# A two-layer decoder trunk: first product's first two units interleaved, six convolution taps moved to TensorE, layer norm read from PSUM

## The chip, the cores and the metric

The kernel runs on one core of one Trainium2 chip. The metric is the device time of one execution in microseconds (us). A core has five engines that run side by side, each with its own queue of instructions, worked off in order: TensorE (PE, matrix products; its weight loads are shown as PEld), VectorE (DVE), ScalarE (ACT), GpSimd (POOL) and SyncE (SP, which here issues the transfers). They work on the on-chip memory SBUF; TensorE writes to PSUM, eight banks of 2 KB a partition, which DVE and ACT can read and write too. An instruction waits on semaphores for what it needs.

## What is computed

The input x is 256 positions by 2048 channels in float32. Cut to what matters here, with the attention of the second layer and both feed-forward stages left as they are:

```python
def _conformer_conv(h, w1, b1, dw, dw_b, ln_g, ln_b, w2, b2):
    u = h @ w1 + b1
    a, gate = jnp.split(u, 2, axis=-1)
    u = a * jax.nn.sigmoid(gate)
    u = lax.conv_general_dilated(u, dw[:, None, :], ...) + dw_b
    u = jax.nn.silu(_layernorm(u, ln_g, ln_b))
    return u @ w2 + b2
...
h = h + _conformer_conv(_rmsnorm(h, a_norm_g), ...)
h = h + _swiglu(_rmsnorm(h, ffn_norm_g), ...)
h = h + _dilated_attention(...) @ w_o
h = h + _swiglu(_rmsnorm(h, ffn_norm_g), ...)
return _rmsnorm(h, final_norm_g)
```

## The kernel before

Activations lie transposed, channels on the 128 partitions: 16 tiles of 128 x 256. Each weight matrix is cut into units (256 output columns) and a unit into blocks of 512 KB: four tiles of 128 input channels. One list, `blocks` (L120 to L143), holds all blocks in the order in which they are used. `emit_block` (L149) loads the next one into `raw` (four buffers, on SP's queue) and parts it into `whi` (float32r, rounded, a copy on ACT) and `wlo` (the rest, a subtraction on DVE or POOL), three buffers each; it runs two blocks ahead of its use. A tile of weights then takes three passes on TensorE: whi with x's high part, whi with x's low part, wlo with x's high part. The first product's first block of a unit is native: float32 weights and float32 x (`rawn`, `xf`, L240) in one pass, which needs no parting.

The first product (w1, line L245) has 16 units of 256 columns, each making a gate tile and a value tile of the same 128 channels. With unit 0 the activations are loaded too: `load_x` (L378) puts a piece of x before each piece of weights on SP's queue, parts x (L292 on ACT, L293 on DVE), and the squares for the RMS norm are summed on POOL, ACT and DVE (L311 to L315). The norm's factor (L318) is applied to the unit's result in PSUM (`glu`, L394). Then the unit's convolution runs while TensorE works on the next units: the taps (`conv`, L406) are shared by POOL and ACT (six products), DVE (the others, L426, accumulating in PSUM), and for the last unit TensorE (16 taps as products with diagonal matrices, L419). `later` and `tick` (L189, L192) deal out these pieces block by block. `stats` (L478) gathers mean and mean square in PSUM by products with a matrix of ones.

The layer norm (L521 to L547) is the seam: it needs all 16 tiles, and its instructions on ACT, DVE and POOL stand in the order in which they are written. It copies the mean to SBUF, subtracts it (DVE for the first two tiles, POOL for the others), multiplies by the reciprocal standard deviation (L537), applies SiLU (L545), and parts the result into z's high and low halves (L546, L547), which the second product (w2, L211 and L216 from here on) reads. Its eight units follow one after the other, each with a tile `pp` of two banks, two such tiles in all.

At the end the last product (wd1, L252) gives its outputs with positions on partitions, in two halves of 128 positions; for its last quarter of the columns the first half is finished first, and `done` (L680) closes the norm and stores it while TensorE makes the second.

The functions that the change touches:

## Time and profile before

| what | us |
|---|---|
| median of the runs (2196.13 to 2197.51) | 2196.61 |
| the profiled execution, its own time | 2197.23 |
| its span, first to last instruction | 2194.4 |
| PE busy | 2166.4 (99%) |
| DVE, ACT, POOL busy | 1378.2, 1063.2, 468.2 |

The span is what the profile's rows are counted in, from 0; 2.8 us of the execution's time lie outside it. A row in order of time has start, length, engine, line, operation, out<-in, shapes, how many instructions were merged and, in brackets, the idle time before and what ended it. Lengths overlap: the next instruction of an engine can start up to 0.1 us before the one ahead has ended, and a matmul's end is modelled, so the distance from start to start tells more. A float32 matmul is two records.

### The profile page before, as it was taken

How to read it: one execution, taken by the hardware profiler on the slowest of the kernel's cores; microseconds unless marked ns; L12 is line 12 of the kernel's file. 1: busy time of each engine (PE TensorE's matmuls, PEld its weight loads, DVE VectorE, ACT ScalarE, POOL GpSimd, SP SyncE). 2: the span in 40 equal slices, each digit the busy share in tenths (PEclk: the TensorE clock that was granted, in tenths of full speed). 3: DMA queues.
4: the chain of work that ended last, by engine and by line, in shares of the span. 5: the costliest groups of instructions: out<-in, count | busy, mean ns of one | idle time of the engine just before them, and what ended most of it. 6: DMA issues, size and time to landing. Idle time of an engine off the chain costs nothing.

```text
span 2194.4 us, 31099 instructions
## 1 busy us (share of the span) xinstructions
PE 2166.4 (99%) x12242; PEld 1903.6 (87%) x12242; DVE 1378.2 (63%) x1634; ACT 1063.2 (48%) x1381; POOL 468.2 (21%) x294
## 2 busy tenths in 40 slices
PE   8999799999999999999999999999999999999998
PEld 7999688888888888888888888888888888888886
DVE  7888876666666565555545677666666566655554
ACT  6666455444444444444444566554444444453333
POOL 5999211222221220000000100112221222210000
PEclk9999899999999999999999999999999999999999
DMA  6444355555555555555565644555655555565654
GB/s 235 168 170 154 105 186 189 183 192 185 191 190 192 192 191 185 191 192 191 178 195 187 192 142 144 183 185 186 191 187 192 192 192 191 185 194 194 196 190 155
DMA packets 112898, 402.40 MB, mean 183 GB/s; under 512 B 12656, under 2 KB 13680, under 8 KB 112752
## 3 DMA queue, kind: packets, MB, share of 16 engines
q1 hardware_dynamic: 111456, 398.30, 55.5%
q8 instruction: 95, 1.56, 0.3%
q10 hardware_dynamic: 1296, 2.12, 0.3%
q14 instruction: 51, 0.42, 0.1%
HBM read 398.28 MB, written 2.10 MB: 182 GB/s over the span
## 4 chain that ended last, share of the span: by engine, by line
PE 97%; DVE 1%; ACT 1%; issue 0%; DMA 0%; POOL 0%; SPq 0%; ACTq 0%; DVEq 0%
PE pp L211 47%; PE pp L216 25%; PE pp L245 8%; PE pp L263 5%; PE pp L265 5%; PE pp L264 5%; PE aux L608 0%; PE aux L613 0%; PE aux L590 0%; PE aux L489 0%; DMA hT<-xT 0%; ACT whi L171 0%; DVE aux L426 0%; PE aux L322 0%; DVE wlo L173 0%
## 5 line engine op out<-in xcount | busy, mean ns | idle before, releaser
L173 DVE TENSOR_TENSOR wlo<-raw,whi 128x1024 fp32r<-128x1024 f32 (+1 forms) x691 | 939.9, 1373 | 504.8 <-ACT whi L171 502.6
L171 ACT CAST whi<-raw 128x1024 fp32r<-128x1024 f32 (+1 forms) x739 | 773.6, 1048 | 789.9 <-PE pp L211 406.0
L211 PE MATMUL pp<-x,whi 128*128 128x512 f32 x3328 | 802.1, 392 | 0.0
L211 PEld LDWEIGHTS pp<-x,whi 128*128 128x128 f32 x3328 | 611.5, 188 | 117.4
L216 PEld LDWEIGHTS pp<-x,wlo 128*128 128x128 f32 x3328 | 426.9, 191 | 16.3
L216 PE MATMUL pp<-x,wlo 128*128 128x256 f32 x3328 | 433.2, 283 | 0.0
L287 DVE TENSOR_TENSOR t<-pp,t 128x512 f32<-128x512 f32 x104 | 71.9, 692 | 208.8 <-ACT t L286 208.8
L286 ACT COPY t<-pp 128x512 f32<-128x512 f32 x104 | 61.2, 588 | 259.8 <-PE pp L211 259.8
L568 POOL TENSOR_TENSOR hid<-t,hid 128x512 fp32r<-128x512 f32 x44 | 89.4, 2031 | 419.8 <-ACT hid L567 419.8
L211 PE MATMUL pp<-hid,whi 128*128 128x512 f32 x704 | 168.7, 391 | 0.0
L211 PEld LDWEIGHTS pp<-hid,whi 128*128 128x128 f32 x704 | 129.2, 188 | 24.9
L426 DVE SCALAR_TENSOR_TENSOR aux<-up,vecs,aux 128x256 f32<-128x256 f32 x355 | 144.7, 485 | 3.3 <-ACT aux L424 3.3
L245 PE MATMUL pp<-x,whi 128*128 128x256 f32 x768 | 143.8, 289 | 1.0 <-ACT whi L171 1.0
L315 POOL TENSOR_TENSOR sqacc<-sqacc,sq 128x512 f32<-128x512 f32 x24 | 36.2, 1507 | 505.6 <-ACT sq L311 505.4
L263 PE MATMUL pp<-whi,hid 128*128 128x512 f32 x352 | 137.8, 392 | 0.8 <-DVE x L669 0.8
L264 PE MATMUL pp<-wlo,hid 128*128 128x512 f32 x352 | 137.1, 389 | 0.4 <-DVE wlo L173 0.4
L265 PE MATMUL pp<-whi,hid 128*128 128x512 f32 x352 | 137.1, 389 | 0.0
L562 POOL TENSOR_TENSOR t<-t,rstd 128x512 f32<-128x512 f32 x44 | 57.0, 1295 | 316.5 <-DVE t L287 316.5
L245 PEld LDWEIGHTS pp<-x,whi 128*128 128x128 f32 x768 | 122.3, 194 | 2.3 <-ACT whi L171 1.4
L173 POOL TENSOR_TENSOR wlo<-raw,whi 128x1024 fp32r<-128x1024 f32 x48 | 114.0, 2389 | 24.4 <-DVE up L398 14.9
L245 PE MATMUL pp<-x,wlo 128*128 128x256 f32 x384 | 110.2, 287 | 3.2 <-DVE wlo L173 3.2
L216 PEld LDWEIGHTS pp<-hid,wlo 128*128 128x128 f32 x704 | 90.8, 191 | 3.7
(134 smaller groups left out, 1870.8 us busy)
## 6 DMA issues: line engine op xcount, KB each, us to landing
raw<-wg SPq DMA_DIRECT2D x176, 512.0 KB, 3.3
raw<-wu SPq DMA_DIRECT2D x176, 512.0 KB, 4.2
raw<-wd SPq DMA_DIRECT2D x176, 512.0 KB, 3.4
raw<-w SPq DMA_DIRECT2D x77, 512.0 KB, 3.2
raw<-wv SPq DMA_DIRECT2D x32, 512.0 KB, 4.0
raw<-wk SPq DMA_DIRECT2D x32, 512.0 KB, 4.2
raw<-wq SPq DMA_DIRECT2D x32, 512.0 KB, 3.4
raw<-wo SPq DMA_DIRECT2D x32, 512.0 KB, 3.3
```

What stands on the lines that cost most here:

```text
L171: nc.scalar.copy(hi[:, part, :], raw[:, part, :])
L173: eng.tensor_tensor(out=lo[:, part, :], in0=raw[:, part, :], in1=hi[:, part, :].bitcast(F32), op=ALU.subtract)
L211: nc.tensor.matmul(bk[:, m, :, :], hi[:, j, ws], x[:, kt, :, :], start=kt == 0, stop=kt == kt_n - 1 and m_last, skip_group_check=True)
L216: nc.tensor.matmul(bk[:, m, 0, :], lo[:, j, ws], x[:, kt, 0, :], start=False, stop=kt == kt_n - 1 and not m_last, skip_group_check=True)
L245: nc.tensor.matmul(bk[:, m, :], a[:, j, ws], b, start=first and m == 0 and i == 0, stop=last and i == len(passes) - 1, skip_group_check=True)
L263: nc.tensor.matmul(o, x[:, kt, 0, ts], hi[:, j, :], start=kt == 0, stop=False)
L264: nc.tensor.matmul(o, x[:, kt, 0, ts], lo[:, j, :], start=False, stop=False)
L265: nc.tensor.matmul(o, x[:, kt, 1, ts], hi[:, j, :], start=False, stop=kt == kt_n - 1)
L286: nc.scalar.copy(t, bk[:, :, 1, :])
L287: nc.vector.tensor_tensor(out=t, in0=bk[:, :, 0, :], in1=t, op=ALU.add)
L426: nc.vector.scalar_tensor_tensor(out=acc[i % 2], in0=win, scalar=w, in1=acc[i % 2], op0=ALU.mult, op1=ALU.add)
L568: nc.gpsimd.tensor_tensor(out=hid[:, 2 * u:2 * u + 2, 1, :], in0=o, in1=hid[:, 2 * u:2 * u + 2, 0, :].bitcast(F32), op=ALU.subtract)
```

## The change

Four things are changed.

1. The list of blocks begins with the first two units of w1 in turns (unit, block): `TURNS`. Both units' results are open at once, the second in a buffer of `aux`. The square sums use POOL for two pairs of x instead of four, unit 1's splits are on DVE, and the results of w1 have two banks instead of three.
2. Tile 14's convolution gives six of its taps to TensorE, with diagonal matrices as for tile 15. The table load for the square root is moved behind the products of tile 15.
3. The layer norm reads mean and reciprocal from the statistics' own PSUM bank (a pool `one` of one bank), DVE subtracts for the tiles 0 to 7 and POOL for 8 to 15, and the first two units of w2 run side by side: their first blocks are native (float32 weights with the float32 result of the SiLU), then their other blocks alternate, the second unit with its narrow pass first. Tiles 0 to 3 of z are parted last.
4. The last product's last quarter has two tiles of `aux` instead of one `pp`, and most of the norm's sum is prepared before it. `aux` has three buffers instead of four from the second product on; the attention's transposes use the bank of `one`.

TensorE at the start, before and after (pp is unit 0's result, aux unit 1's; rawn are native weights; L322 and L362 are the norm's sums):

```order
1 L245 MATMUL pp<-xf,rawn 128x256 x8
2 L245 MATMUL pp<-x,whi 128x256 x2
3 L245 MATMUL pp<-x,wlo 128x256
...
50 L322 MATMUL aux<-sqacc,cst 128x256 x2
51 L245 MATMUL pp<-xf,rawn 128x256 x8
```
```order
1 L259 MATMUL pp<-xf,rawn 128x256 x8
2 L259 MATMUL aux<-xf,rawn 128x256 x8
3 L259 MATMUL pp<-x,whi 128x256 x2
4 L259 MATMUL pp<-x,wlo 128x256
...
19 L259 MATMUL aux<-x,whi 128x256 x2
20 L259 MATMUL aux<-x,wlo 128x256
...
67 L362 MATMUL aux<-sqacc,cst 128x256 x2
```

Unit 1's native block stands second and its first split block (rows 19 on) ahead of unit 0's third block; its last two blocks come after row 67.

DVE at the layer norm, before and after (cT holds the 16 tiles, st the statistics in PSUM, rstd the factor; L533 and L608 are the reciprocal):

```order
185 L526 TENSOR_TENSOR rstd<-mu 128x256 [waits Activation_49]
186 L527 TENSOR_TENSOR rstd<-aux,rstd 128x256 [waits DVE_49,PE_49]
187 L532 TENSOR_TENSOR cT<-cT,mu 128x256 x2
188 L533 RECIPROCAL rstd<-rstd 128x256 [waits Activation_49]
189 L537 TENSOR_TENSOR cT<-cT,rstd 128x256 [waits DVE_49]
190 L537 TENSOR_TENSOR cT<-cT,rstd 128x256
191 L547 TENSOR_TENSOR z<-cT,z 128x256 [waits DVE_49,Activation_49]
192 L537 TENSOR_TENSOR cT<-cT,rstd 128x512 [waits Pool_49]
```
```order
171 L586 TENSOR_TENSOR cT<-cT,st 128x256 [waits PE_49,Activation_49]
172 L603 TENSOR_TENSOR rstd<-st,rstd 128x256
173 L586 TENSOR_TENSOR cT<-cT,st 128x256
174 L608 RECIPROCAL st<-rstd 128x256 [waits DVE_49,Activation_49]
175 L591 TENSOR_TENSOR cT<-cT,st 128x256 [waits DVE_49]
176 L591 TENSOR_TENSOR cT<-cT,st 128x256
177 L586 TENSOR_TENSOR cT<-cT,st 128x512
178 L591 TENSOR_TENSOR cT<-cT,st 128x512 [waits DVE_49]
```

Every one of DVE's operands that was mu or rstd in SBUF is now st in PSUM; z is parted only after row 182, and the wait for POOL stands later.

TensorE from the last taps into the second product, before and after (diag are the taps' matrices, L489, L493 and L539, L543 the statistics):

```order
877 L419 MATMUL aux<-up,diag 128x256 x15
878 L489 MATMUL aux<-cT,cst 128x256 [waits DVE_49]
879 L493 MATMUL aux<-sq_2607,cst 128x256 [waits Activation_49]
...
882 L211 MATMUL pp<-z,whi 128x512 [waits DVE_49,PE_49]
883 L211 MATMUL pp<-z,whi 128x512
884 L211 MATMUL pp<-z,whi 128x512 [waits DVE_49]
```
```order
824 L463 MATMUL aux<-up,diag 128x256 x5
...
881 L463 MATMUL aux<-up,diag 128x256 x15
882 L539 MATMUL st<-cT,cst 128x256 [waits DVE_49]
883 L543 MATMUL st<-sq_2626,cst 128x256 [waits Activation_49]
...
886 L272 MATMUL pp<-cT,rawn 128x256 [waits DMAHW4_49,PE_49,Activation_49]
...
888 L272 MATMUL pp<-cT,rawn 128x256 [waits Activation_49]
...
896 L284 MATMUL pp<-z,whi 128x512 [waits DVE_49]
...
900 L282 MATMUL pp<-z,wlo 128x256 [waits Pool_49]
```

Tile 14's six taps stand 57 rows earlier, among unit 15's matmuls; the second product now begins with matmuls that wait for ACT's SiLU alone, and DVE's parted z is first waited for in row 896.

The core of the diff:

```diff
-TAPS_OF = [(6, 0)] * 14 + [(6, 0), (3, 16)]
+TAPS_OF = [(6, 0)] * 14 + [(6, 6), (3, 16)]
...
-    for u in range(DT):
+    TURNS = ((0, 0), (1, 0), (0, 1), (1, 1), (0, 2), (0, 3), (1, 2), (1, 3))
+    blocks.extend((w1, u, g, GK) for u, g in TURNS)
+    for u in range(2, DT):
         plan(w1, u, DT)
-    for u in range(DT // 2):
+    for g in range(DT // GK):
+        blocks.extend((w2, u, g, GK) for u in range(2))
+    for u in range(2, DT // 2):
...
-        native = NATIVE if w is w1 and g == 0 else 0
+        native = NATIVE if g == 0 and (w is w1 or w is w2 and u < 2) else 0
...
-                eng = nc.gpsimd if (w is w1 and i >= 6) or (w is w2 and u == 0) else nc.vector
+                eng = nc.gpsimd if (w is w1 and u > 1) or (w is w2 and u < 2 and (u, g) in ((0, 1), (1, 1), (0, 2))) else nc.vector
...
+    one = ctx.enter_context(tc.tile_pool(name="one", bufs=1, space=PSUM))
...
-        return psum[-1].tile(shape, F32, name="aux", bufs=4 if len(psum) > 1 else 5)
+        return psum[-1].tile(shape, F32, name="aux", bufs=3 if len(psum) > 1 else 5)
...
+        bks = [aux([P, 2, S]) if i else psum[-1].tile([P, 2, S], F32, name="pp", bufs=2) for i in range(len(units))]
+        for u, g in TURNS if len(units) > 1 else [(0, g) for g in range(DT // GK)]:
+            raw, hi, lo = next_block(w, units[u], g)
...
+    def project_pair(w, xf, x, bks):
+
+        parts = [next_block(w, u, 0, 0)[0] for u in range(2)]
+        for s in range(0, GK, 2):
+            for bk, raw in zip(bks, parts):
+                for kt in (s, s + 1):
+                    for m in range(2):
+                        nc.tensor.matmul(bk[:, m, 0, :], raw[:, kt, m * P:(m + 1) * P], xf[:, kt, :], start=kt == 0, stop=False,
+                                         skip_group_check=True)
+            yield
+        for g in range(1, DT // GK):
+            for u, bk in enumerate(bks):
+                hi, lo = next_block(w, u, g, 0)[1:]
+                tiles = [(g * GK + j, j, m, slice(m * P, (m + 1) * P)) for j in range(GK) for m in range(2)]
+                for wide in ((True, False), (False, True))[u]:
+                    for kt, j, m, ws in tiles:
+                        if not wide:
+                            nc.tensor.matmul(bk[:, m, 0, :], lo[:, j, ws], x[:, kt, 0, :], start=False, stop=False, skip_group_check=True)
+                        else:
+                            nc.tensor.matmul(bk[:, m, :, :], hi[:, j, ws], x[:, kt, :, :], start=False, stop=kt == DT - 1,
+                                             skip_group_check=True)
+                yield
...
+        if done:
+            outs = [aux([P, NBV]) for _ in range(2)]
+        else:
+            bk = bank2()
+            outs = [bk[:, t, :, :].rearrange("p a b -> p (a b)") for t in range(2)]
...
-                norm.add(hT[:, j:j + 2, :], *((nc.gpsimd, nc.gpsimd) if j < DT // 2 else (nc.scalar, nc.vector)))
+                norm.add(hT[:, j:j + 2, :], *((nc.gpsimd, nc.gpsimd) if j < 4 else (nc.scalar, nc.vector)))
...
+            pe_acc = acc[-1]
+            begun = n_pe > 0 and j < DT - 1
...
-                if i < 2:
+                if i < 2 and not (i and begun):
...
+        table(AF.Sqrt, last_product[-1])
+        for _ in range(3):
+            emit_block()
...
+        bks = [bank2(), bank2()]
+        pair = project_pair(w2, cT, z, bks)
...
+            def centred(j, n, eng, m):
+                c2 = cT[:, j:j + n, :]
+                eng.tensor_tensor(out=c2, in0=c2, in1=_bc(m, n), op=ALU.subtract)
+
+            def scaled(j, n):
+
+                c2 = cT[:, j:j + n, :]
+                nc.vector.tensor_tensor(out=c2, in0=c2, in1=_bc(st[:, 1, :], n), op=ALU.mult)
+                for q in range(j, j + n):
+                    nc.scalar.activation(cT[:, q, :], cT[:, q, :], AF.Silu, bias=v("ln_b", q), scale=v("ln_g", q))
+
+            def parted(j, n):
+                nc.vector.tensor_copy(z[:, j:j + n, 0, :], cT[:, j:j + n, :])
+                nc.vector.tensor_tensor(out=z[:, j:j + n, 1, :], in0=cT[:, j:j + n, :], in1=z[:, j:j + n, 0, :].bitcast(F32), op=ALU.subtract)
...
+            nc.scalar.activation(rl, st[:, 0, :], AF.Square)
             nc.scalar.copy(mu, st[:, 0, :])
-            rl = sp.tile([P, S], F32, name="rstd")
-            nc.vector.tensor_tensor(out=rl, in0=mu, in1=mu, op=ALU.mult)
+            centred(*groups[0], nc.vector, st[:, 0, :])
             nc.vector.tensor_tensor(out=rl, in0=st[:, 1, :], in1=rl, op=ALU.subtract)
             nc.scalar.activation(rl, rl, AF.Sqrt, bias=ln_eps)
-            groups = [(0, 1), (1, 1)] + [(j, 2) for j in range(2, DT, 2)]
-            for j, n in groups:
-                c2 = cT[:, j:j + n, :]
-                (nc.vector if j < 2 else nc.gpsimd).tensor_tensor(out=c2, in0=c2, in1=_bc(mu, n), op=ALU.subtract)
-            nc.vector.reciprocal(rl, rl)
-
-            def scaled(j, n):
-                c2 = cT[:, j:j + n, :]
-                nc.vector.tensor_tensor(out=c2, in0=c2, in1=_bc(rl, n), op=ALU.mult)
-
-            scaled(*groups[0])
+            centred(*groups[1], nc.vector, st[:, 0, :])
+            for j, n in groups[5:]:
+                centred(j, n, nc.gpsimd, mu)
+            nc.vector.reciprocal(st[:, 1, :], rl)
             for i, (j, n) in enumerate(groups):
-                if i + 1 < len(groups):
-                    scaled(*groups[i + 1])
-                c2 = cT[:, j:j + n, :]
-                for q in range(n):
-                    nc.scalar.activation(c2[:, q, :], c2[:, q, :], AF.Silu, bias=v("ln_b", j + q), scale=v("ln_g", j + q))
-                (nc.scalar.copy if n == 1 else nc.vector.tensor_copy)(z[:, j:j + n, 0, :], c2)
-                nc.vector.tensor_tensor(out=z[:, j:j + n, 1, :], in0=c2, in1=z[:, j:j + n, 0, :].bitcast(F32), op=ALU.subtract)
-
-        conv_psum.close()
-        psum.append(ctx.enter_context(tc.tile_pool(name="ps", bufs=1, space=PSUM)))
-        x, norm = out_proj(w2, DT, z, "b2", "f0_g")
+                if 2 <= i < 5:
+                    centred(j, n, nc.vector, st[:, 0, :])
+                scaled(j, n)
+                if j in (1, 2):
+                    next(pair)
+                if j >= 8:
+                    parted(j - 4, 2)
+                if j == 10:
+                    next(pair)
+                    next(pair)
+            emit_block()
+            parted(12, 2)
+            next(pair)
+            parted(14, 2)
+            next(pair)
+            emit_block()
+            emit_block()
+            next(pair)
+            next(pair)
+            parted(0, 2)
+            parted(2, 2)
+
+        x, norm = out_proj(w2, DT, z, "b2", "f0_g", bks)
...
+        for t in range(2):
+            r = ss[t][:, 4:5]
+            nc.vector.tensor_reduce(out=r, in_=ss[t][:, 0:3], axis=AX.X, op=ALU.add)
+            nc.vector.tensor_scalar(out=r, in0=r, scalar1=1.0 / D, scalar2=RMS_EPS, op0=ALU.mult, op1=ALU.add)
 
         def done(t, p):
             c = D // NBV - 1
             add(c, t, p)
-            r = ss[t][:, 4:5]
-            nc.vector.tensor_reduce(out=r, in_=ss[t][:, 0:4], axis=AX.X, op=ALU.add)
-            nc.scalar.activation(r, r, AF.Sqrt, scale=1.0 / D, bias=rms_eps)
+            r = ss[t][:, 5:6]
+            nc.scalar.activation(r, ss[t][:, c:c + 1], AF.Sqrt, scale=1.0 / D, bias=ss[t][:, 4:5])
             nc.vector.reciprocal(r, r)
```

More of the change, by code (lines that the diff above doesn't have):

```diff
@@ L181, in next_block @@
         assert blocks[i][:3] == (w, u, g)
-        while len(ready) < min(len(blocks), i + 1 + AHEAD):
+        while len(ready) < min(len(blocks), i + 1 + ahead):
             emit_block()
@@ L605, in transpose @@
             def transpose():
[L606 removed]
+                pt = one.tile([P, 3, P], F32, name="pt", tag="one")
                 for a in range(3):
```

93 lines of the change are left out of this document (53 added, 40 removed).

## The prediction

> **What bounds the kernel now.** I read the page first, then who waited for whom on TensorE, then stretches with the granted clock, then rows in order of time at three places. TensorE is busy 99% of the span and waits in few places:
>
> ```profile
> PE 2166.4 (99%) x12242; PEld 1903.6 (87%) x12242; DVE 1378.2 (63%) x1634; ACT 1063.2 (48%) x1381; POOL 468.2 (21%) x294
> ```
> ```profile
> PE pp L211 <- DVE z L547: 10.7, 3, 9.3
> PE pp L245 <- DVE xf L382: 3.7, 1, 3.7
> PE pp L245 <- DVE wlo L173: 3.2, 3, 2.3
> ...
> PE pp L263 <- DVE x L669: 0.8, 1, 0.8
> ```
>
> The largest wait (10.7 us) is the layer norm's, the next ones are the start's, the last is at the end. A wait costs more than its length, as the stretches show (columns: length, busy time of PE, PEld, DVE, ACT, POOL, granted clock, DMA share, GB/s):
>
> ```profile
> 9.80:14.20 4.40, 1.04 (x4) 0.64 (x4) 4.25 (x4) 4.33 (x10) 4.32 (x4) 0.80 1.04 390
> 14.20:19.60 5.40, 5.12 (x25) 4.83 (x25) 5.40 (x9) 4.86 (x12) 1.85 (x2) 0.53 1.04 416
> ...
> 100.00:200.00 100.00, 100.00 (x722) 96.24 (x721) 87.45 (x221) 64.27 (x125) 94.19 (x59) 1.00 0.48 166
> 224.30:227.70 3.40, 1.17 (x5) 0.59 (x4) 1.65 (x4) 1.29 (x3) 1.44 (x1) 0.96 0.00 0
> 227.70:235.00 7.30, 0.00 (x0) 0.01 (x1) 7.27 (x7) 3.30 (x6) 7.30 (x7) 0.50 0.00 0
> 235.00:244.60 9.60, 8.09 (x26) 6.25 (x27) 8.93 (x13) 6.19 (x11) 2.77 (x2) 0.50 0.01 2
> ```
>
> Behind both idle stretches TensorE works at half its clock for 5 to 10 us. Between 100 and 200 us TensorE is never idle, and POOL (94%) and DVE (87%) are close behind it.
>
> **Start.** In order of time on TensorE, then ACT, then DVE:
>
> ```profile
> 3.69 6.31 PE L245 MATMUL pp<-xf,rawn 128*128 128x256 f32 x16 [3.69 <-DVE xf L382]
> ...
> 25.25 1.13 PE L322 MATMUL aux<-sqacc,cst 128*128 128x256 f32 x4
> 26.22 3.62 PE L245 MATMUL pp<-xf,rawn 128*128 128x256 f32 x16
> ...
> 39.84 3.19 PE L245 MATMUL pp<-xf,rawn 128*128 128x256 f32 x14
> ```
> ```profile
> 9.41 0.91 ACT L292 ACTIVATE x<-hT,vecs 128x256 fp32r<-128x256 f32 x2 [6.73 <-DMA hT<-xT]
> ...
> 16.69 0.89 ACT L292 ACTIVATE x<-hT,vecs 128x256 fp32r<-128x256 f32 x2
> 17.49 0.60 ACT L171 CAST whi<-raw 128x512 fp32r<-128x512 f32 x1
> ```
> ```profile
> 9.95 2.17 DVE L293 SCALAR_TENSOR_TENSOR x<-hT,vecs,x 128x256 fp32r<-128x256 f32 x2 [2.61 <-ACT x L292]
> ...
> 16.94 0.87 DVE L293 SCALAR_TENSOR_TENSOR x<-hT,vecs,x 128x256 fp32r<-128x256 f32 x2
> ...
> 26.93 1.75 DVE L325 RECIPROCAL rstd<-rstd 128x256 f32<-128x256 f32 x1 [1.73 <-ACT rstd L324]
> ```
>
> Unit 0 ends at 25.25, unit 1 at 39.84 (less 0.4, two matmuls of unit 2 being done by then). The native block (16 records) takes 6.31 us at the first clock, 3.4 later. A whole unit is 12.51 us by the two gate products:
>
> ```profile
> 201.85 0.70 DVE L395 TENSOR_TENSOR pp<-pp,rstd 128x512 f32<-128x512 f32 x1 [1.39 <-PE pp L245]
> ...
> 214.36 0.70 DVE L395 TENSOR_TENSOR pp<-pp,rstd 128x512 f32<-128x512 f32 x1 [1.00 <-PE pp L245]
> ```
>
> Less 3.4 of native block and 0.4 of statistics that makes 2.9 us for each of the three split blocks. The change puts unit 1's native block and its first split block (6.3 us) ahead of unit 0's third. What this meets: (a) 1 MB more weights land before the last x, 2.6 us at 390 to 416 GB/s. The ninth transfer on the queue is now 512 KB, not 256, so x's third pair lands near 11.0, not 9.4 (estimate from 256 KB at 237 to 390 GB/s and the rows' order). (b) From there ACT is the chain: six pairs of x at 0.80 (row to row, 16.69 to 17.49), and, by the half cast of 0.60 that overlaps its neighbours by 0.1, six half casts at 0.5, four squares of the same size at 0.5, and one whole cast at 1.0 make 10.8, so its last cast ends near 22, with some waiting. (c) DVE's 2.17 against 0.87 for the same two instructions is POOL's doing, busy 4.32 of 4.40 us there; the change leaves POOL two squares and one addition, so DVE's extra work (two additions of squares at 0.7, as the 128x512 multiplication at 236.82 below, and one whole split, twice that) fits, the last split ending near 23. (d) TensorE then has native work until 13.3, is held up little, and has work without a gap from unit 1's split at 16.9: 2.9, then two blocks of unit 0, 2.9 each: it ends unit 0 at about 25.4, as early as before, if the clock, now without an idle stretch, stays up. Then 0.9 for the norm's matmuls, 2.9 for a block, 0.4 of waiting for a split that stands behind the reciprocal on DVE (1.75), 2.7 for the rest: unit 1 ends at 32.4 instead of 39.4. Lead 7.0; I take 6.5 for the uncertain landing. Bounds: 4.0 if all of the 2.6 us of transfers delays unit 0, 8.0 if TensorE never idles after 3.69.
>
> **Conv stage.** Nothing is cheaper there: a unit stays 12.51 us of TensorE. The lead is kept if the helpers keep up.
>
> ```profile
> L173 POOL TENSOR_TENSOR wlo<-raw,whi 128x1024 fp32r<-128x1024 f32 x48 | 114.0, 2389 | 24.4 <-DVE up L398 14.9
> ```
>
> POOL needs 11.8 us a unit (94.19 of 100): three splits of 2.4 and 4.6 for the rest. Unit 1's two splits go from it to DVE. The narrowest place is the last block of unit 2: from about 29, when the first cast for POOL is done, two splits, unit 0's additions and the third split end at 29 + 4.8 + 4.6 + 2.4 = 40.8, and TensorE is there at 32.4 + 3.4 + 2 x 2.9 = 41.6. DVE needs 10.9 a unit of 12.5. Cost 0; bound 3 us of waits.
>
> **Six taps.** The last stages of the convolution:
>
> ```profile
> 216.28 7.18 PE L419 MATMUL aux<-up,diag 128*128 128x256 f32 x32 [0.23 <-DVE up L398]
> ...
> 225.16 0.61 PE L493 MATMUL aux<-sq,cst 128*128 128x256 f32 x2
> 235.03 1.19 PE L211 MATMUL pp<-z,whi 128*128 128x512 f32 x2 [9.26 <-DVE z L547]
> ```
> ```profile
> 223.61 0.95 DVE L462 TENSOR_TENSOR cT<-aux,cT 128x256 f32<-128x256 f32 x2
> ```
>
> Sixteen taps take 7.18, so six take 2.6 (7.18 / 32 records x 12), and they stand among unit 15's matmuls, where TensorE has no slack: +2.6, with nothing to hide it. The diagonals' extra copies on ACT are hidden (64% busy). DVE loses five taps of unit 14, but its order has ten of them behind unit 15's gate product where six stood; at 0.41 a tap (144.7 busy us for 355) I get its last addition 10.9 us behind that product instead of 10.2 (214.36 to 224.56): +0.7, bounds -0.2 and +2.5.
>
> **Layer norm.** From the end of the statistics at 225.77:
>
> ```profile
> 234.80 1.76 DVE L537 TENSOR_TENSOR cT<-cT,rstd 128x512 f32<-128x512 f32 x1
> ...
> 236.82 0.68 DVE L537 TENSOR_TENSOR cT<-cT,rstd 128x512 f32<-128x512 f32 x1
> ...
> 263.75 0.88 DVE L346 SCALAR_TENSOR_TENSOR hT<-pp,vecs,hT 128x256 f32<-128x256 f32 x2 [1.45 <-PE pp L211]
> ```
> ```profile
> 232.10 0.60 ACT L545 ACTIVATE cT<-cT,vecs 128x256 f32<-128x256 f32 x1 [3.09 <-DVE cT L537]
> ```
> ```profile
> 361.06 1.91 PE pp L216 x16
> 362.97 3.65 PE pp L211 x16
> ```
>
> The same multiplication takes 1.76 us while POOL runs and 0.68 after it. With an operand in PSUM it isn't slowed: the gate product above, on PSUM, takes 0.70 with POOL at 94%. The new chain: Square and copy on ACT 0.9 (0.91 for two such above), subtraction and variance on DVE 0.9 (0.95 for two additions above), root 0.45, reciprocal 1.75 (as at 26.93), multiplication 0.4, SiLU 0.6, handovers 0.1: first matmul 5.1 us behind the statistics instead of 9.26. DVE's subtraction waits for ACT's two reads of the same bank. The Trainium skill ("PSUM — Partial Sum Buffer", section "PSUM bank collisions raise a hardware error") says that ScalarE and VectorE may not read one bank at once, which is why; no run here shows a collision. The Trainium skill speaks against the whole move ("VectorE: DVE Perf Modes", section "Rules for kernel authors": for many operations on a matmul's output, copy it to SBUF first); by that the wait would stay at 9.26, by the rows here it is 5.1.
>
> Then 16 native matmuls need no split z: 6.8 us for two blocks. Steady split blocks take 2.78 (1.91 + 3.65 for two), so native costs 1.3 more; six split blocks make 16.7. The half clock costs half of the time it lasts: 9.6 us before, where the work comes with gaps; at the start, with few gaps, it is over 5.4 us after work resumes (14.20 to 19.60), so 2.7 now. Plus 0.3 for the third unit's bank, which DVE frees behind a split. Units 0 and 1 end 5.1 + 6.8 + 16.7 + 2.7 + 0.3 = 31.6 behind the statistics, against 263.75 - 225.77 = 38.0: gain 6.4. Bounds: 3.5 (half clock twice as long) and 9 (no half clock).
>
> **End.**
>
> ```profile
> 2188.28 0.16 DVE L684 TENSOR_REDUCE ss<-ss 128x1 f32<-128x4 f32 x1
> ```
>
> Two tiles instead of one take away TensorE's wait for DVE's read of the first half (0.8, above), and one reduction of 0.16 leaves the last chain, 0.2 with its handover: 1.0, bounds 0.8 and 1.2. In the attention one bank fewer is shared by scores and values, and the transposes have one bank:
>
> ```profile
> L609 ACT COPY pT<-aux x16: 457/480/489, 1269.8 to 1369.5; 128x384 f32<-128x384 f32 x16
> ```
>
> The second head's transposes now wait for the first's copy (0.48), under which three to seven other matmuls of 0.12 to 0.23 lie: 0, bound 1.
>
> **Sum.** 6.5 - 2.6 - 0.7 + 6.4 + 1.0 = 10.6 off the profiled execution's 2197.23, which is 0.6 above the median of the runs: 2186.0 against 2196.61.
>
> **Rivals.** The fourth rests on the taps' row:
>
> ```profile
> L426 DVE SCALAR_TENSOR_TENSOR aux<-up,vecs,aux 128x256 f32<-128x256 f32 x355 | 144.7, 485 | 3.3 <-ACT aux L424 3.3
> ```
>
> 1. Unit 0 doesn't end as early: the 2.6 us of transfers pass through to ACT's chain. For: transfers run at 390 to 416 GB/s there. Against: TensorE had 4.4 us idle in them. Gain 8.0: 2188.6. Chance 0.12.
> 2. The lead is used up: POOL at 94% can't start earlier than it did, so TensorE waits until POOL's old timetable. For: 0.8 us of room at unit 2. Against: its splits wait for whi buffers that now come free earlier. 6.5 less: 2192.5. Chance 0.09.
> 3. The clock stays up through the layer norm. Against: 224.30 to 227.70 held 1.17 us of matmuls and the clock still fell. 2.7 more: 2183.3. Chance 0.08. The Trainium skill ("TensorE: Matmul & The Clock Gate", section "What's actually happening") lets it fall after an idle window of about 3.4 us, free-running, by which an idle stretch of 5 us may pass between two windows.
> 4. Slower: DVE becomes the bound of the conv stage. Two units' taps reach it within 7 us, with two banks for the products where three were, so a late gate product stops the unit after next. It decides from a DVE unit above 12.8 us (6.5 of lead lost and 13 x 0.32). At the taps' own length of 485 ns, rather than its share of the busy time, 0.41, a unit is 13.35: 6.5 + 13 x 0.84 lost, 2203.4. Against: 87.45 of 100. Chance 0.05.
> 5. The second head's copy stands behind a whole cast on ACT (1.0) in all eight pairs: 8.0 more, 2194.0. Chance 0.04.
>
> **Numbers.** The forecast has 0.62, with 2181 to 2190 by the bounds of its terms. The range 2181 to 2192.5 takes in rivals 1 to 3 and leaves out 4, 5 and the tails. A measurement of this kernel tells 0.2% (4.4 us) from no change: faster means below 2192.2. The forecast, rivals 1 and 3 and half of 2 give 0.87; the rest of 2 and rival 5 give 0.09; rival 4 gives 0.04.
>
> **What would show it.** Right: unit 1's end near 32.4, no half clock at 13 to 19 us, unit 15's gate product near 210, the first native matmul of the second product 5 us behind the statistics, DVE's multiplications at 0.4 and 0.7 beside POOL, no wait ahead of the last half. Wrong: TensorE waiting for wlo from POOL between 35 and 60 us, gate products ending a unit late, or a wait of TensorE for z.

## The result and the profile after

The changed kernel takes 2184.86 us (median of 2184.23 to 2185.62), the kernel before 2196.61 (2196.13 to 2197.51): a ratio of 0.9946 (95% interval 0.993 to 0.9962), 11.75 us less where 10.6 were forecast. The profiled execution took 2185.62 with a span of 2183.8, so the span shrank by 10.6 us (the other three executions of the changed kernel had spans of 2182.4 to 2183.4). The other 1.0 us by which the two profiled executions differ lies around the span: it was 2.83 us in the profiled execution before and 1.8 after, and in further runs of the kernel before it was anything from 1.74 to 3.0.

Who waited for whom on TensorE in the changed kernel (columns: us in total, times, longest):

```profile
PE pp L272 <- ACT cT L593: 5.0, 1, 5.0
PE pp L259 <- DMA rawn<-w: 3.7, 1, 3.7
PE st L539 <- DVE cT L511: 1.0, 1, 1.0
PE aux L259 <- DVE wlo L178: 0.4, 2, 0.3
```

The layer norm's wait is 5.0 instead of 10.7, that for the last half is gone, and nothing waits for POOL. The start in order of time on TensorE, then stretches with the clock (columns as before: length, PE, PEld, DVE, ACT, POOL, clock, DMA share, GB/s):

```profile
3.71 6.00 PE L259 MATMUL pp<-xf,rawn 128*128 128x256 f32 x16 [3.71 <-DMA rawn<-w]
9.97 3.72 PE L259 MATMUL aux<-xf,rawn 128*128 128x256 f32 x16 [0.26 <-DMA rawn<-w]
13.34 0.59 PE L259 MATMUL pp<-x,whi 128*128 128x256 f32 x2
...
25.84 1.03 PE L362 MATMUL aux<-sqacc,cst 128*128 128x256 f32 x4
...
33.18 3.62 PE L259 MATMUL pp<-xf,rawn 128*128 128x256 f32 x16
```
```profile
9.80:14.20 4.40, 4.23 (x22) 3.82 (x23) 2.32 (x5) 2.89 (x7) 0.00 (x0) 1.00 1.03 391
14.20:19.60 5.40, 5.10 (x40) 4.69 (x39) 5.38 (x11) 5.40 (x12) 0.00 (x0) 1.00 1.05 410
...
227.80:230.30 2.50, 2.50 (x6) 2.04 (x7) 2.43 (x5) 1.72 (x4) 0.73 (x1) 0.50 0.00 0
230.30:232.80 2.50, 2.50 (x7) 1.94 (x7) 2.43 (x5) 2.27 (x5) 0.00 (x0) 0.50 0.00 0
232.80:235.30 2.50, 2.50 (x11) 2.12 (x10) 2.47 (x6) 1.78 (x4) 0.00 (x0) 0.82 0.00 0
```

TensorE worked 4.23 us between 9.8 and 14.2 instead of 1.04, at full clock, and unit 2 begins at 33.18. The half clock behind the layer norm is still there, to about 233.7 (0.82 over the last 2.5 us is 0.9 us more of it); it began at about 226.8, inside the wait:

```profile
222.80:227.80 5.00, 0.05 (x2) 0.02 (x1) 3.97 (x7) 3.11 (x6) 4.21 (x4) 0.90 0.00 0
```

(0.90 over 5.0 us is 1.0 us at half clock.) The convolution's end, the layer norm and the tail, on DVE and TensorE:

```profile
210.74 0.70 DVE L435 TENSOR_TENSOR pp<-pp,rstd 128x512 f32<-128x512 f32 x1 [1.63 <-PE pp L259]
...
220.68 0.95 DVE L511 TENSOR_TENSOR cT<-aux,cT 128x256 f32<-128x256 f32 x2
...
227.34 0.68 DVE L586 TENSOR_TENSOR cT<-cT,st 128x512 f32<-128x512 f32 x1
228.06 0.69 DVE L591 TENSOR_TENSOR cT<-cT,st 128x512 f32<-128x512 f32 x1
...
254.62 0.88 DVE L386 SCALAR_TENSOR_TENSOR hT<-pp,vecs,hT 128x256 f32<-128x256 f32 x2 [0.19 <-PE pp L284]
...
2172.36 0.69 DVE L750 TENSOR_TENSOR x<-aux,x 128x512 f32<-128x512 f32 x1 [1.77 <-PE aux L305]
...
2176.44 0.69 DVE L750 TENSOR_TENSOR x<-aux,x 128x512 f32<-128x512 f32 x1 [0.87 <-PE aux L305]
```
```profile
222.22 0.61 PE L543 MATMUL st<-sq,cst 128*128 128x256 f32 x2
227.78 10.07 PE L272 MATMUL pp<-cT,rawn 128*128 128x256 f32 x32 [4.95 <-ACT cT L593]
237.50 2.19 PE L284 MATMUL pp<-z,whi 128*128 128x512 f32 x8
```

Set beside the kernel before, point by point, this is where the time went. A unit's gate product is DVE's first instruction on its finished result (`pp<-pp,rstd`), its residual the one that adds the second product's result to h (`hT<-pp,vecs,hT`); the times are starts, for the statistics the end:

| point | before | after | gained so far |
|---|---|---|---|
| unit 2 begins (less 0.4 done early, before) | 39.42 | 33.18 | 6.2 |
| unit 15's gate product | 214.36 | 210.74 | 3.6 |
| statistics end | 225.77 | 222.83 | 2.9 |
| first matmul of the second product | 235.03 | 227.78 | 7.25 |
| its unit 1's residual | 263.75 | 254.62 | 9.1 |
| its unit 2's residual | 274.88 | 266.02 | 8.9 |
| TensorE's second last half read | 2181.64 | 2172.36 | 9.3 |
| its last half read | 2186.82 | 2176.44 | 10.4 |
| span | 2194.4 | 2183.8 | 10.6 |

The step from 8.9 to 9.3 happens between 1270 and 1460 us, in the attention; from unit 2's residual to the last product the difference moves nowhere else. The first row differs between executions by up to 0.8 us on each side: with the same start, unit 2 begins at 32.6 to 33.3 in the eight traces of the changed kernel and its variants, and at 39.4 to 40.2 in the three of the kernel before and its variants.

### The profile page after: what moved, and what is told of

The parts are those of the page before. It is cut to its first block, busy times and chain, and to the rows that moved or that the text cites. A ratio compares the mean times of both kernels' runs of the same rounds, so it can differ in the third digit from the quotient of the medians.

```text
span 2183.8 us, 31131 instructions
## 1 busy us (share of the span) xinstructions
PE 2165.4 (99%) x12254; PEld 1904.9 (87%) x12254; DVE 1368.0 (63%) x1636; ACT 1062.1 (49%) x1385; POOL 452.2 (21%) x284
## 4 chain that ended last, share of the span: by engine, by line
PE 97%; DVE 1%; ACT 0%; issue 0%; DMA 0%; SPq 0%; POOL 0%; ACTq 0%; DVEq 0%
PE pp L217 47%; PE pp L222 25%; PE pp L259 8%; PE pp L304 4%; PE pp L303 4%; PE pp L305 4%; PE aux L305 1%; PE aux L304 1%; PE aux L303 1%; PE pp L284 1%; PE pp L272 0%; DVE aux L470 0%; PE aux L694 0%; PE aux L671 0%; PE pt L689 0%
## 5 line engine op out<-in xcount | busy, mean ns | idle before, releaser
L217 PEld LDWEIGHTS pp<-x,whi 128*128 128x128 f32 x3328 | 611.2, 188 | 117.3
L222 PE MATMUL pp<-x,wlo 128*128 128x256 f32 x3328 | 433.3, 283 | 0.0
L259 PE MATMUL pp<-x,whi 128*128 128x256 f32 x720 | 133.5, 287 | 0.0
L259 PEld LDWEIGHTS pp<-x,whi 128*128 128x128 f32 x720 | 113.3, 192 | 0.9
L178 POOL TENSOR_TENSOR wlo<-raw,whi 128x1024 fp32r<-128x1024 f32 x45 | 107.2, 2406 | 23.0 <-ACT whi L176 23.0
L303 PE MATMUL pp<-whi,hid 128*128 128x512 f32 x264 | 103.5, 392 | 0.0
L304 PE MATMUL pp<-wlo,hid 128*128 128x512 f32 x264 | 102.9, 390 | 0.3 <-DVE wlo L178 0.3
L305 PE MATMUL pp<-whi,hid 128*128 128x512 f32 x264 | 102.8, 390 | 0.0
L259 PE MATMUL pp<-x,wlo 128*128 128x256 f32 x360 | 101.9, 283 | 0.1
```

The costliest lines, as they stand in the source:

```text
L178: eng.tensor_tensor(out=lo[:, part, :], in0=raw[:, part, :], in1=hi[:, part, :].bitcast(F32), op=ALU.subtract)
L217: nc.tensor.matmul(bk[:, m, :, :], hi[:, j, ws], x[:, kt, :, :], start=kt == 0, stop=kt == kt_n - 1 and m_last, skip_group_check=True)
L222: nc.tensor.matmul(bk[:, m, 0, :], lo[:, j, ws], x[:, kt, 0, :], start=False, stop=kt == kt_n - 1 and not m_last, skip_group_check=True)
L259: nc.tensor.matmul(bks[u][:, m, :], a[:, j, m * P:(m + 1) * P], b, start=kt == 0 and m == 0 and i == 0, stop=kt == DT - 1 and i == len(pas ...
L303: nc.tensor.matmul(o, x[:, kt, 0, ts], hi[:, j, :], start=kt == 0, stop=False)
L304: nc.tensor.matmul(o, x[:, kt, 0, ts], lo[:, j, :], start=False, stop=False)
```

## The experiments

The number in brackets is the distance to the kernel before, run on the same chip beside it (2195.89, 2196.42 or 2196.87); the changed kernel's is -11.75. The changed kernel was not run again beside them, and the kernel before differs by up to 1.0 us between these sets, so a small distance between a run and the changed kernel is given twice, by the medians and by these distances.

**1. The start.** `start_seq`: the changed kernel, units 0 and 1 one behind the other.

```
-TURNS = ((0, 0), (1, 0), (0, 1), (1, 1), (0, 2), (0, 3), (1, 2), (1, 3))
+TURNS = tuple((u, g) for u in range(2) for g in range(4))
```

> The changed kernel, with the first product's unit 0 done in full before unit 1, as before; all else of the change is kept. Theory (the lead of 6.2 us comes from TensorE having unit 1's blocks to do while unit 0's x arrives): TensorE stands idle again between 10 and 14 us and runs at half its clock behind that, unit 1's last matmul ends near 39.4 instead of 33.2, and the whole is 6.2 us longer than the changed kernel, 2191.1. Rival (the start got faster because POOL no longer multiplies squares beside DVE, or because more splits went to DVE): unit 1 ends by 36, the whole is at most 2.5 us longer, 2185 to 2187.5.

2192.69 us (-3.20). Unit 2 begins at 37.02, neither near 39.4 nor before 36: only 3.8 us are lost at the start, and the clock there stays at 1.00. In the profiled executions unit 15's gate product is 9.3 us later than in the changed kernel: 3.8 from the start, the rest from a stall of its own at 65 us with the clock halved behind it. By the second product's unit 2, 2.5 us of this have come back (its residual is 6.8 later). Unit 1's gate product, which has lower priority in this code, comes late in DVE's order there (43.55); I take that for the cause of the stall, but it was not tried apart. The waits of TensorE in `start_seq`:

```profile
PE st L539 <- POOL cT L552: 3.9, 1, 3.9
...
PE pp L259 <- ACT whi L176: 2.7, 1, 2.7
```

So taking turns is worth 3.8 of the 6.2 us; something else carries the other 2.4. `pool_sq` and `bef_sq` look for it in the squares, from both sides:

```
(pool_sq, in the changed kernel)
-  *((nc.gpsimd, nc.gpsimd) if j < 4 else (nc.scalar, nc.vector))
+  *((nc.gpsimd, nc.gpsimd) if j < DT // 2 else (nc.scalar, nc.vector))
(bef_sq, in the kernel before: the same line the other way round)
```

> The changed kernel with x's first eight pairs of rows squared and added on POOL, as before, instead of the first four. Theory (POOL's work beside DVE slows DVE's remainders of x, 2.17 us for two instead of 0.88, and x is what unit 0 waits for): TensorE waits 1.5 to 3 us more for x and wlo between 12 and 25 us, unit 1 ends at 34.7 to 36.2 instead of 33.2, the whole is 1.5 to 3 us longer. Rival (unit 1's blocks cover it, and ACT and DVE have two squares and two additions less): unit 1 ends within 0.5 us of 33.2, the whole is the same.

> The kernel before, with only the squares of x's rows 4 to 7 moved from POOL to ACT and their additions to DVE, as in the change. Theory (a part of the start's gain is DVE freed from POOL, with units 0 and 1 still one behind the other): DVE's first remainders take 0.88 us instead of 2.17, TensorE's idle stretch before 14 us shrinks from 4.4 to under 3 us, its clock does not halve behind it, unit 1 ends 2 to 2.5 us earlier than 39.4, and the whole is 2 us shorter than the kernel before. Rival (ACT, busy 4.33 of 4.40 us there, passes on the two squares): unit 1 ends within 0.7 us of 39.4, and the whole is the same.

`pool_sq`: 2187.61 (-8.81), unit 2 begins at 35.91, 2.7 us later, as its theory had it. On its DVE, then on its TensorE:

```profile
11.66 2.18 DVE L333 SCALAR_TENSOR_TENSOR x<-hT,vecs,x 128x256 fp32r<-128x256 f32 x2 [4.43 <-ACT x L332]
13.76 1.75 DVE L178 TENSOR_TENSOR wlo<-raw,whi 128x512 fp32r<-128x512 f32 x1
...
19.77 0.87 DVE L333 SCALAR_TENSOR_TENSOR x<-hT,vecs,x 128x256 fp32r<-128x256 f32 x2
```
```profile
15.57 0.39 PE L259 MATMUL pp<-x,wlo 128*128 128x256 f32 x1 [1.58 <-DVE wlo L178]
...
18.77 0.39 PE L259 MATMUL pp<-x,wlo 128*128 128x256 f32 x1 [1.52 <-DVE wlo L178]
```

Beside POOL's squares, up to 17.8 us, DVE takes 2.18 and 1.75 for what takes 0.87 and 0.68 without them. `bef_sq`: unit 2 begins at 36.73, 2.7 us earlier than before. The two agree: squares 2.7, turns 3.8, together 6.5 against the 6.2. But the whole of `bef_sq` is only 1.1 us shorter, where 2 were expected, and that is not clear of noise (2195.30, ratio 0.9995, interval 0.9986 to 1.0004). Its last gate product comes 2.3 us earlier, and DVE's last addition then ends 11.7 us behind it instead of 10.2: DVE's queue gives most of the lead back.

**2. The taps.** `no_taps`: the changed kernel without the six taps; `best`: with two more on the last unit (and with the filling matmuls of part 3).

```
-TAPS_OF = [(6, 0)] * 14 + [(6, 6), (3, 16)]
+TAPS_OF = [(6, 0)] * 14 + [(6, 0), (3, 16)]      (no_taps)
+TAPS_OF = [(6, 0)] * 14 + [(6, 6), (3, 18)]      (best)
```

> The changed kernel without the six taps of unit 14 on TensorE: all of its taps are DVE's and ACT's again. In DVE's order 31 taps then stand behind unit 15's gate product instead of 20. Theory (DVE's order sets the end of the convolution, so the six taps buy more than their 2.6 us): the gate product comes 2.6 us earlier, 208.1, DVE's last addition 4.5 us later behind it (11 more taps at 0.41), 15.4 us, so the statistics end 1.9 us later and the whole is 2186.8. Rival (the taps only cost, since DVE finished 10.2 us behind the gate product before the change with all taps): the last addition comes 10.2 us behind the gate product, the whole is 3.3 us shorter, 2181.6.

> The run warm11 (11 filling matmuls) with 18 instead of 16 taps of the last unit on TensorE. DVE has two taps (0.8 us) less behind the last gate product, TensorE two taps (0.9 us) more, where it waited 1.0 us for DVE. Theory (DVE's order ends the convolution): the last addition comes 10.05 to 10.2 us behind the gate product instead of 10.9, and the whole is 0.5 to 0.8 us shorter than warm11, 2181.9 to 2182.2. Rival (TensorE's taps now end last): no gain.

`no_taps`: 2187.51 (-8.38), 2.7 to 3.4 us longer than the changed kernel. On its DVE:

```profile
208.03 0.70 DVE L435 TENSOR_TENSOR pp<-pp,rstd 128x512 f32<-128x512 f32 x1 [1.37 <-PE pp L259]
...
210.07 7.92 DVE L470 SCALAR_TENSOR_TENSOR aux<-up,vecs,aux 128x256 f32<-128x256 f32 x20
...
222.54 0.95 DVE L511 TENSOR_TENSOR cT<-aux,cT 128x256 f32<-128x256 f32 x2
```

The gate product comes 2.7 us earlier, and the last addition ends 15.5 us behind it (15.4 expected) instead of 10.9; the rival falls. DVE waited 1.37 us for that gate product and did 20 taps after it: its order, not its speed, holds the lag. The statistics end 2.8 us later than in the changed kernel, not the expected 1.9: TensorE waited 3.30 us for DVE, and its clock was at half (from about 222.0) for the last of them. `best`: 2182.33 (-14.54), the fastest of all, but only 0.3 us below `warm11` (0.8 by the distances). Its last addition ends 10.4 us behind the gate product, where 10.05 to 10.2 were expected, since it now waits for TensorE's taps:

```profile
220.88 0.42 DVE L511 TENSOR_TENSOR cT<-aux,cT 128x256 f32<-128x256 f32 x1 [0.42 <-PE aux L463]
```

**3. The layer norm.** `ln_sbuf`: the changed kernel with DVE's mean and reciprocal root in SBUF. `warm` and `warm11`: the changed kernel with TensorE's wait filled. `warm_sbuf`: both, with 13.

```
-nc.vector.reciprocal(st[:, 1, :], rl)        ... in1=_bc(st[:, 1, :], n), op=ALU.mult
+nc.vector.reciprocal(rl, rl)                 ... in1=_bc(rl, n), op=ALU.mult     (the mean: mu for st[:, 0, :])
...
 bks = [bank2(), bank2()]
+idle = aux([P, S])
+for i in range(22):                          (warm11: 11; warm_sbuf: 13)
+    nc.tensor.matmul(idle, ones, cst[:, 0:S], start=True, stop=True)
```

> The changed kernel, with the layer norm's mean and reciprocal root read by DVE from SBUF instead of PSUM; nothing else moves. Theory (an operand in PSUM spares DVE the slowdown beside POOL): DVE's subtractions and multiplications take up to 2.5 times as long while POOL subtracts, as the 1.76 us against 0.68 of the kernel before; the first native matmul of the second product comes 6.5 to 7.5 us behind the statistics instead of 4.95, and the whole is 1.5 to 3 us longer, 2186.4 to 2187.9. Rival (an operand in SBUF is as fast or faster for DVE): 4.7 to 5.0 us, and the whole within 0.3 us of the changed kernel.

> The changed kernel with 22 matmuls of 128x256 more between the layer norm's statistics and the second product; they read constants, write a PSUM bank that nobody reads, and fill TensorE's wait of 4.95 us at 0.216 each (4.75 us). Theory (the clock halves because TensorE idles, and that costs half of the 5.9 us that it lasts): the granted clock stays at 1.00 from 227.8 on, the two native blocks take 6.8 us instead of 9.7, and the whole is 2.5 to 3.0 us shorter, 2181.9 to 2182.4. Rival (the wait behind is not TensorE's clock but the order in which DVE and ACT hand over cT's pieces): the native blocks still end near 237, the whole is within 0.7 us of the changed kernel.

`ln_sbuf`: 2185.64 (-10.25), the profiled span 2183.5 against 2183.8. Its first matmul did come later (5.86 us behind the statistics instead of 4.95), since DVE's first two multiplications took 2.33 beside POOL instead of 0.75. But in the two profiled executions the native blocks end equally late behind the statistics, 14.66 us and 14.67 in the changed kernel. The stretches show why:

```profile
226.72 2.33 DVE L591 TENSOR_TENSOR cT<-cT,rstd 128x256 f32<-128x256 f32 x2
```
```profile
228.34 9.15 PE L272 MATMUL pp<-cT,rawn 128*128 128x256 f32 x32 [5.86 <-ACT cT L593]
237.14 2.19 PE L284 MATMUL pp<-z,whi 128*128 128x512 f32 x8
```
```profile
225.60:228.30 2.70, 0.00 (x0) 0.00 (x0) 2.67 (x3) 0.80 (x2) 2.70 (x3) 0.50 0.00 0
227.80:230.30 2.50, 1.96 (x5) 1.60 (x6) 2.47 (x3) 1.09 (x2) 0.97 (x1) 0.50 0.00 0
230.30:232.80 2.50, 2.50 (x9) 2.00 (x8) 2.43 (x5) 2.14 (x4) 0.00 (x0) 0.58 0.00 0
232.80:235.30 2.50, 2.50 (x13) 2.22 (x12) 2.47 (x6) 2.12 (x5) 0.00 (x0) 1.00 0.00 0
```

The half clock lasted to about 232.4, 4.1 us from the first matmul instead of 5.9. Neither theory had this. But it had also begun earlier, at about 225.5: it lasted 6.8 us, as in the changed kernel (226.8 to 233.7), and only more of it fell into the wait. Nothing ties that to the operands. In `start_seq`, whose layer norm is that of the changed kernel and whose wait is 4.95 us too, the clock fell only as the work resumed, stayed at half for 3.4 us, and the native blocks took 8.5 us instead of 9.7:

```profile
235.79 8.84 PE L272 MATMUL pp<-cT,rawn 128*128 128x256 f32 x32 [4.95 <-ACT cT L593]
244.28 2.19 PE L284 MATMUL pp<-z,whi 128*128 128x512 f32 x8
```
```profile
230.80:235.80 5.00, 0.05 (x2) 0.01 (x1) 3.96 (x7) 3.10 (x6) 4.20 (x4) 1.00 0.00 0
235.80:239.20 3.40, 3.40 (x8) 2.77 (x9) 3.30 (x6) 2.62 (x5) 0.74 (x1) 0.50 0.00 0
239.20:241.70 2.50, 2.50 (x13) 2.19 (x13) 2.47 (x6) 2.09 (x5) 0.00 (x0) 1.00 0.00 0
```

So one pair of profiled executions can't tell what the operands are worth behind a half clock. By all runs `ln_sbuf` is 0.8 us longer than the changed kernel by the medians and 1.5 by the distances: at most the low end of the theory, and more than the rival's 0.3. `warm`: 2186.68 (-9.21), slower than the changed kernel, because the filling was mis-sized: a matmul of 128x256 in f32 is two records of 0.216, so 22 filled 9.5 us. The clock held, though: 1.00 in every stretch, and the native blocks took 6.72. So the size was halved:

> As the run warm, with 11 matmuls instead of 22: one such matmul took 0.432 us there (two records of 0.216), so 11 fill 4.75 of the 4.95 us that TensorE waits. Theory (the clock halves because TensorE idles): the native blocks begin 4.95 to 5.1 us behind the statistics as in the changed kernel, take 6.7 us instead of 9.7, and the whole is 2.4 to 3.0 us shorter than the changed kernel, 2181.9 to 2182.5. Rival (DVE's and ACT's hand-over of cT and z comes too late to feed a faster TensorE): waits appear ahead of the blocks of the second product, and the whole is under 1 us shorter.

```profile
222.50 4.91 PE L580 MATMUL aux<-cst 128*128 128x256 f32 x22
227.61 7.17 PE L272 MATMUL pp<-cT,rawn 128*128 128x256 f32 x32 [0.20 <-ACT cT L596]
234.43 2.18 PE L284 MATMUL pp<-z,whi 128*128 128x512 f32 x8
```

`warm11`: 2182.65 (-13.77; ratio 0.9937, interval 0.9922 to 0.9951). The first native matmul is as early behind the statistics as in the changed kernel (4.95), the blocks take 6.8 instead of 9.7, and no wait appears behind them: the half clock cost 2.9 us in that execution, and idling causes it. The whole is 2.2 us shorter by the medians and 2.0 by the distances, less than the 2.4 to 3.0 expected. What the half clock costs differs from one execution to the next (1.7 us in `start_seq`, 8.5 against 6.8), and the profiled execution of the changed kernel was the longest of its four.

> The run ln_sbuf (mean and reciprocal root in SBUF) with 13 filling matmuls of 0.432 us (5.6 us of its wait of 5.9). Theory (in ln_sbuf the first matmul came 0.9 us later, but the half clock behind it lasted 4.1 us instead of 5.9, which gave the same 0.9 back; with the clock held up nothing gives it back): the native blocks take 6.8 us, and the second product stands 0.9 us later behind the statistics than in warm11. Rival (the later pieces of cT and z, not the first, pace the second product): no difference to warm11 at unit 2's residual.

`warm_sbuf`: 2184.08 (-12.79). The rows of `warm_sbuf`, then of `warm11`:

```profile
228.34 1.13 PE L272 MATMUL pp<-cT,rawn 128*128 128x256 f32 x4 [0.26 <-ACT cT L596]
229.74 6.31 PE L272 MATMUL pp<-cT,rawn 128*128 128x256 f32 x28 [0.27 <-ACT cT L596]
264.22 0.88 DVE L386 SCALAR_TENSOR_TENSOR hT<-pp,vecs,hT 128x256 f32<-128x256 f32 x2 [1.45 <-PE pp L217]
```
```profile
262.91 0.88 DVE L386 SCALAR_TENSOR_TENSOR hT<-pp,vecs,hT 128x256 f32<-128x256 f32 x2 [1.44 <-PE pp L217]
```

Behind the statistics its unit 2's residual stands 1.5 us later than in `warm11` (41.75 against 40.25 us), more than the 0.9 of the theory: 0.9 at the first matmul and the rest in the blocks, whose second part waits 0.27 us for the slow multiplications. With the clock held up, the operands in PSUM are worth 1.5 us there, and the whole agrees (1.4 by the medians, 1.0 by the distances).

`bef_psum` puts only the operands into PSUM, in the kernel before; `bef_psum1` also gives their bank a pool of its own, with one shared tile fewer.

```
-nc.vector.reciprocal(rl, rl)                   ... in1=_bc(rl, n), op=ALU.mult
+nc.vector.reciprocal(st[:, 1, :], rl)          ... in1=_bc(st[:, 1, :], n), op=ALU.mult     (the mean of tiles 0 and 1: st[:, 0, :] for mu)
...
-st = aux([P, 2, S])                            (bef_psum1 only)
+st = one.tile([P, 2, S], F32, name="st")       (and aux with bufs 4 and 3 for 5 and 4)
```

> The kernel before, with only the layer norm's mean and reciprocal root read by DVE from PSUM instead of SBUF. Theory (after the run with SBUF operands in the changed kernel, where the first matmul came 0.9 us later but the blocks ended at the same time): DVE's multiplications take 0.7 instead of 1.76, the first matmul of the second product comes 1.5 to 2.5 us earlier than 9.26 behind the statistics, but DVE's remainders of z, which have no operand in PSUM, and the half clock behind the wait hold the rest: unit 1's residual (263.75) comes at most 1 us earlier. Rival (the operands in PSUM are themselves most of the 6.2 us): 3 us or more.

> As bef_psum (the kernel before, mean and reciprocal root read from PSUM), but the bank that holds them has a pool of its own, so that the second product's banks do not lie on it; the other small PSUM tiles share four banks instead of five (three instead of four from the second product on). Theory (the 17.8 us that TensorE waited in bef_psum were for that bank, which DVE read until its last multiplication): the first matmul of the second product waits for z alone, which came 5.95 us behind the statistics there, so it starts 6.0 instead of 9.26 us behind them. DVE's whole chain ended 5 us earlier in bef_psum, so unit 1's residual comes 3 to 4.5 us earlier than the kernel before (263.75), and the whole is 3 to 4.5 us shorter than it, 2191.9 to 2193.4. Rival (as the run ln_sbuf suggests, operands in PSUM shorten DVE's chain, but the half clock behind the wait takes it back): the first matmul starts near 6 us, and the residual comes less than 1.5 us earlier.

`bef_psum`: 2201.77 (+5.35), slower, which neither theory had. TensorE's first matmul, of `bef_psum`, then of `bef_psum1`:

```profile
244.38 3.75 PE L211 MATMUL pp<-z,whi 128*128 128x512 f32 x8 [17.82 <-DVE cT L537]
```
```profile
232.07 2.55 PE L212 MATMUL pp<-z,whi 128*128 128x512 f32 x4 [6.09 <-DVE z L548]
```

In `bef_psum` it waits 17.8 us for DVE's last multiplication: the second product's banks lie where the statistics' bank was, and that bank is now read to the end. With a bank of its own (`bef_psum1`, 2193.87, -3.00) the wait is 6.1, as expected, and unit 1's residual comes 35.5 us behind the statistics instead of 38.0: 2.4 us earlier, between the two theories. The first matmul alone is 3.2 us earlier than the 9.26 of the kernel before. Waits between the pieces of z (TensorE waits 1.9 us for the second) and the half clock (0.50 to 240, 0.74 from 240 to 245) lie behind it; how the lost 0.7 splits between them was not tried.

**4. The end and the attention.** `end_att`:

```
-pt = one.tile([P, 3, P], F32, name="pt", tag="one")
+pt = aux([P, 3, P])
...
-    outs = [aux([P, NBV]) for _ in range(2)]    (if done; now both halves of bank2() always)
```

> The changed kernel with the attention's transposes in the shared PSUM tiles again (three banks instead of four), and the last product's two halves in one tile again; the prepared sum of squares stays. Theory: TensorE waits 0.8 us for DVE's read of the first half, the last half ends 1.0 to 1.1 us later against the first than in the changed kernel (4.1 us between DVE's two additions, 5.2 before); and the 0.4 us that the stretch of the attention had lost come back, since its transposes wait for other tiles. The whole is 1.2 to 1.5 us longer, 2186.1 to 2186.4. Rival (the attention's 0.4 us are from elsewhere): the attention stays as in the changed kernel, and the whole is 1.0 us longer.

2186.71 (-10.16). The last two halves:

```profile
2172.16 0.69 DVE L749 TENSOR_TENSOR x<-pp,x 128x512 f32<-128x512 f32 x1 [1.77 <-PE pp L304]
...
2177.32 0.69 DVE L749 TENSOR_TENSOR x<-pp,x 128x512 f32<-128x512 f32 x1 [1.96 <-PE pp L304]
```

The last half comes 5.16 us behind the half ahead of it (4.08 in the changed kernel): 1.08 us, as expected. Through the attention it loses 0.73 us against the changed kernel, more than the 0.4, so the rival falls. That it is more fits its having one shared tile fewer than the kernel before as well; this was not tried apart.

## Why the prediction was right, and where it was off

The sum of the forecast, 10.6, is what the span lost, and that is partly luck: the start and the layer norm gave 0.8 less than forecast, the attention and the end 0.7 more.

- **Start, 6.5 forecast, 6.2 measured.** The native work ended at 13.34 (13.3 forecast), the last cast on ACT at 22.4 (22), DVE's last split at 23.5 (23), unit 0 at 25.84 (25.4), unit 1 at 33.18 (32.4). Of rival 1, transfers that delay unit 0, at most 0.6 us of its 2.6 can have come: unit 0 ends that much later than before. The 6.5 was a lead of 7.0 less 0.5 for an uncertain landing. What the working put in passing, that DVE is freed of POOL, turned out to be 2.7 of the 6.2 (`pool_sq`, `bef_sq`). The clock stayed up, as the working asked, but not for the turns' sake: in `start_seq`, without them, it stays up too.
- **Conv stage, 0 and 0.** From unit 5 to unit 14 every gate product is 6.23 earlier (101.74 against 95.51 for unit 6, for instance), and no wait for POOL appears on TensorE: rivals 2 and 4 did not come.
- **Six taps, -2.6 and -2.6; DVE's end, -0.7 and -0.7** (10.9 us behind the gate product, as read from the order). The working's own quotient for the taps, 7.18 / 32 x 12, is 2.7, not 2.6. The prediction counted the taps as a cost; `no_taps` shows that they buy more than they cost, because the lead would otherwise leave 31 taps behind the last gate product.
- **Layer norm, 6.4 and 5.9.** First matmul 4.95 us behind the statistics (5.1), native blocks 9.7 (9.5), unit 1's residual 31.8 (31.6); 0.3 of it is gone again by unit 2. Operands in PSUM alone gave 2.4 in the kernel before (`bef_psum1`); the other 3.5 are left for the native blocks, the two units in turns and the new order on ACT, DVE and POOL, which were not tried alone, so this part of the account is argued. Rival 3, the clock staying up, did not come by itself. Its price, 2.7, was near the 2.9 that `warm11` measured, but by luck: behind the same wait of 4.95 us the half clock cost 1.7 in `start_seq`. The step on operands in PSUM was right in its durations (0.75 and 0.69 beside POOL, 2.33 with SBUF). What it is worth in the changed kernel as it stands is known only roughly, 0.8 to 1.5 us by `ln_sbuf`; with the clock held up it is 1.5 us (`warm_sbuf`). The Trainium skill ("VectorE: DVE Perf Modes", "Rules for kernel authors") offers, for many operations on a matmul's output, to copy it from PSUM to SBUF first. Beside a working POOL these runs don't bear that out: with the clock held up, operands in SBUF cost the 1.5 us.
- **Attention, 0 forecast (bound 1), +0.4 measured.** The step named the wait for the one bank and left out the other side: the transposes no longer take one of the shared tiles. `end_att` prices the bank at 0.73. Rival 5, a loss of 8.0, did not come.
- **End, 1.0 and 1.3**: 1.1 from the two tiles (0.8 forecast) and 0.2 from the sum.
- Outside the sum, 1.0 us lies around the span. Runs of the kernel before scatter there by 1.3 us, those of the changed kernel by 0.1; what takes the scatter away stays open. `end_att`, with one tile for the last two halves as before, does not scatter either (1.74 to 1.82), so the two tiles are not it.

## What to carry to other kernels

Price an idle stretch of TensorE with the half clock behind it: 5 us of waiting cost 1.7 to 2.9 more here, by where the clock's steps fell, and 11 matmuls into an unread bank took that back. Don't judge such a change by one profiled execution on each side: the same two kernels can be level in one pair and about 1 us apart by all their runs (`ln_sbuf`). Where an engine's order is fixed, look at what stands behind its last awaited instruction before spending on a lead: 2.3 us of lead left 0.8 at the statistics in `bef_sq`. And ask of a bank that constants are read from what is laid on it next.

## What the runs showed of the hardware

- The clock's half stretches behind the layer norm lasted 3.4 us (`start_seq`, 235.8 to 239.2), 6.8 (the changed kernel, 226.8 to 233.7; `ln_sbuf`, 225.5 to 232.4) and 17.1 (the kernel before, 227.4 to 244.5): one, two and five times 3.4. They began 5.0, 4.0 and 3.1 us after TensorE had begun to wait in `start_seq`, the changed kernel and `ln_sbuf`. So the same wait of 4.95 us was followed by 3.4 or by 5.9 us of work at half clock, and a longer one of 5.86 by 4.1. Idle stretches of 2.2 us (`bef_sq`) and 2.7 (`start_seq`) left the clock at 1.00, one of 3.9 (`start_seq`, at 65 us) did not. The Trainium skill ("TensorE: Matmul & The Clock Gate", "What's actually happening") has a free-running window of about 3.4 us. The stretches here agree with it.
- DVE beside POOL lost a factor of 2.5 to 3.1 on two-operand work with all operands in SBUF (0.87 to 2.18, 0.75 to 2.33), and nothing when one was in PSUM (two of 128x256 in 0.75, one of 128x512 in 0.69). It is not only two-operand work: in the kernel before, a cast of 128x512 from SBUF to SBUF took 2.35 us beside POOL's split (at 243.15) and 0.42 without, while a reciprocal of 128x256 took 1.74 beside POOL (at 229.37) and 1.75 away from it (at 26.93).
